# Attention units in three parts, and readers set behind their transfers, in a hybrid decoder layer

## The chip, the cores and the metric

One core of a Trainium2 chip runs the whole kernel. The metric is device time in microseconds, from the start of the program to its end. The engines are TensorE (PE, with PEld for its weight loads), VectorE (DVE), ScalarE (ACT), GpSimd (POOL) and SyncE (SP), whose queue issues almost all DMAs.

## The reference, cut to what matters

One layer for 2048 prompt rows and 64 sample rows (8 samples of 8 rows), model width 1024. A normalised row is projected once to 3584 columns. Four groups of 128 channels go through a gated MLP over chunks of 128 rows (mixer A), eight heads of 64 through an attention with three dilation patterns (mixer B). Both are normalised, gated, concatenated and projected; then a second gate is added.

```
for (w, r) in ((128, 1), (512, 4), (2048, 16)):      # window, dilation
    s = q . k * SCALE on banded blocks of 128 x 256   # rows t attend to t, t-r, ..., t-w
    p = exp(s - max(s)); den = sum(p)
    o = p @ v / den; lse = max(s) + log(den)
b_out = softmax(lse over the three patterns) . o
y = x + concat(a_out, norm(b_out) * silu(z)) @ w_out  # then a gate and a per-layer embedding
```

The samples attend in the same three patterns to a cache of 2048 rows and to their own new rows.

## The kernel before, in words

All products of the prompt are made in float16 halves: a value is split into a high half and a residual, and two or three matmuls add up their products.

**Projection.** The columns are taken in eight chunks, in the order A0, B0, B1, A1, B2, B3, A2, A3: an A chunk (384 columns) is a channel group, a B chunk (512 columns) a pair of heads. In each chunk 17 tiles of rows pass, sixteen of 128 prompt rows and as the last one the sample rows (`gemm`, L433). The sample tile keeps both halves of its rows in one tile of 128 partitions, so its product has to be folded (`fold`, L448): ScalarE copies the lower 64 rows to SBUF, a DMA moves them to the upper partitions, and VectorE adds. PSUM has three banks for these products, two for scores, two for values, one for transposes.

**Keys and queries.** Behind every fourth tile of a B chunk GpSimd normalises queries and keys (`b_norm`, L493), and `b_trans` (L532) splits them and transposes them by four DMAs from SyncE into `qk2`, one buffer for the pair of heads that is under way. The next pair may be written only when the pair before is done; the loop over tiles (L1342 to L1352) holds its groups until then, and at the eighth tile it runs the planner until `done` says so.

**Attention units.** A pair of heads has 40 units (`attn`, L642): 4 of pattern 1 and 4 of pattern 2 for each group of four tiles, and 8 of pattern 3 behind the last group, so 160 in all. A unit's first part (`scores`, L688) is two or four pairs of score matmuls, the masked maximum on VectorE (L704), the exponent on ScalarE (L712), the split in two halves on VectorE (L715, L716), and the DMA transpose of the probabilities `pc` into `pT` (L718), issued by SyncE. The second part (`stage_c`, L721) is six or twelve value matmuls (L739 to L741) and a copy by ScalarE into `rec`; a set of units (four, in pattern 3 two) fills one `rec`, which then goes to DRAM. `vload` (L628) reads the values of a set for patterns 2 and 3. `pc` and `pT` have three buffers each, `rec` two, the values three.

**Joining.** `combine` (L755) loads the three patterns' results and the gate for 512 rows, weighs them by their denominators on VectorE, ScalarE and GpSimd and stores the rows for the output phase; four joinings follow each pair of heads, as units without a second part.

**The planner.** The order of the work is written down by `Pump` (L55). It keeps a clock of its own, in ns of estimated TensorE time. Each two matmuls of a projection give it credit (0.6 ns for each ns), and it spends the credit on units: a second part when it is due, `P_LAG` (8000) behind its first part, else a first part while fewer than three wait for their second. A unit's first part is not before `QK_LAG` (3000) behind its key transposes. `later` puts a step (the mixing of an A group) at a due time. Work of the samples (`all_samples`) comes when no unit waits. `run` lets its clock run on without projections.

The framework's scheduler then makes each engine's queue from this program: it goes by the program's order, and by its own estimate of when an instruction is ready; `behind()` keeps the value matmuls behind the last projection matmul that was written ahead of them. On the chip each engine works through its queue in that order.

**Output phase.** Behind the eighth chunk 17 tiles pass through two projections of 1024 columns and one of 256 (`p3_load`, `p3_cat`, `p3_out`, `p3_gate`, `p3_ple`), with the samples' attention in between.

Of the kernel before, what the change touches and what calls it, by code (L numbers as in the profile page):

```python
# [21 lines left out]
P = 128  # L22
# [22 lines left out]
W_V3 = 3000.0  # L45
QK_LAG = 3000.0
P_LAG = 8000.0
MIX_LAG = 12000.0
# [6 lines left out]
class Pump:  # L55
# [4 lines left out]

    def __init__(self, depth, lag):
        self.depth, self.lag = depth, lag
        self.now = 0.0
        self.n = 0
        self.due = []
        self.units = []
        self.pend = []
# [9 lines left out]

    def unit(self, start, first, second):
        self.units.append((start, first, second))

# [3 lines left out]

    def _free(self):

        return self.units and (len(self.pend) < self.depth if self.units[0][2] else not self.pend)

    def _step(self):
        if self.pend and self.pend[0][0] <= self.now:  # L90
            cost = self.pend.pop(0)[1]()
        elif self._free() and self.units[0][0] <= self.now:
            _, first, second = self.units.pop(0)
            cost = first()
            if second:
                self.pend.append((self.now + cost + self.lag, second))
        elif self.units or self.pend or not self.back or self.ready > self.now:
# [22 lines left out]
    def run(self, until):  # L120
        while not until():
            if self._step() is None:
                t = []
                if self.pend:
                    t.append(self.pend[0][0])
                if self._free():
                    t.append(self.units[0][0])
                if not t:
                    assert self.back
# [6 lines left out]
def tile_hymba_gmlp_dilated_attn_step(  # L136
# [30 lines left out]
    drm = ctx.enter_context(tc.tile_pool(name="drm", bufs=1, space=DRAM))  # L167
    pump = Pump(3, P_LAG)
    uid = [0]
# [263 lines left out]
    def gemm(j, wt, ncol):  # L433
        g = pst("g", 3)
        n = 0
        for kt in range(KT):
# [3 lines left out]
            for l, r in ((lh, a), (lh, b), (xT[j][:, KT + kt], a)) if j < NT else ((lh, a), (lh, b)):  # L440
# [3 lines left out]
                if n % 2 == 0:  # L444
                    pump.tick(2 * (ncol * 0.416 + 5))
        return g if j < NT else fold(g, ncol, "tmpA")
# [191 lines left out]

    done = {}
    v_open = []  # L640

    def attn(hp, sc, grp):  # L642
# [17 lines left out]
        for pat, g, sub in steps:  # L660
            o = {}

            def first(pat=pat, g=g, sub=sub, o=o):
                if sub[0][0] == 0:
                    if pat != 1:
                        vload(hp, pat, g)
                    rec[pat] = wk.tile([P, 4, 2, RW], F32, name=nm("rec"), tag="rec", bufs=2)
                o["r"] = rec[pat]
                o["pT"], cost = scores(Q, KH, KL, o["r"], sub)
                return cost  # L670

            def second(pat=pat, g=g, sub=sub, o=o):
                with behind():
                    cost = stage_c(hp, pat, g, sub, o["r"], o["pT"])
                if pat == 1 and (sub[0][0] == 0 and g or sub[0][0] == 3 and g == 3):
                    v_open.pop(0)
                return cost
            pump.unit(start, first, second)
        if grp is None:
            for jg in range(4):  # L680
                def comb(jg=jg):
                    combine(hp, jg, sc)
                    done[hp] = jg == 3
                    return 0.0
                pump.unit(start, comb, None)


    def scores(Q, KH, KL, r, sub):  # L688
# [27 lines left out]
        nc.vector.tensor_tensor(pc[:, n:2 * n], smv, pc[:, :n], op=ALU.subtract)  # L716
        pT = wk.tile([P, 8, P], F16, name=nm("pT"), tag="pT", bufs=3)
        nc.sync.dma_start(pT[:, :2 * n // P, :], pc[:, :2 * n], transpose=True)  # L718
        return pT, 4 * ns * (kw * 0.416 + 8)

# [33 lines left out]

    def combine(hp, jg, sc):  # L755
        rows = lambda t, w: t[jg * 512:(jg + 1) * 512, 0:w].rearrange("(j p) c -> p j c", p=P)
# [5 lines left out]
        gz = wk.tile([P, 4, P], F32, name=nm("gzl"), tag="gzl", bufs=1)  # L762
        nc.sync.dma_start(gz, rows(zscr[hp], P))
        e = small(24, "e24", 2).rearrange("p (i a) -> p i a", i=3)
        nb = [t[:, :, HD + 1] for t in rr]
# [101 lines left out]
    def gemm2(o, nk, wt, m, order=((0, 0), (0, 1), (1, 0), (1, 1))):  # L867
        gs = [pst("g", 3), pst("s", 2)]
        n = [0, 0]
        for part, hf in order if m == P else ((0, 0), (0, 1)):  # L870
            for kt in range(nk):
                w = wt[(kt // 2) * 2 + hf]
                for half in range(2 - part):
# [3 lines left out]
                    if n[hf] % 2 == 0:  # L877
                        pump.tick(2 * 218.0)
        return gs if m == P else [fold(g, 512, "rl", 3) for g in gs]

# [390 lines left out]
    for _ in w0:  # L1271
        pass
    for ci, (kind, i) in enumerate(order):
        wt, sc, ncol = chunks[kind, i]
# [9 lines left out]
        for j in range(NT + 1):  # L1284
# [23 lines left out]
            if j == 6 and ci + 1 < len(order):  # L1308
                gain_load(*order[ci + 1])
            if j % 4 == 0:  # L1310
                mk = b_group if kind == "B" else a_group
                G = mk(i, j // 4, 4, P) if j < NT else mk(i, 4, 1, TS)
            g = gemm(j, wt, ncol)
# [3 lines left out]
            else:  # L1317
                for _ in range(LAST_PREP[j]):
                    if next(nxt, None):
                        break  # L1320
                if j == 14:
                    ring["cat"].append(q4t([P, D], F32, "cat"))
                    ring["x"].append(q4t([P, D], F32, "x3"))
                    p3_load(0)
                elif j == 15:
                    p3_cat(0)
            if kind == "B":
                b_evac(G, j % 4, g, sc)
            else:
                a_evac(G, j % 4, g, sc)  # L1330
            if j % 4 == 3 or j == NT:
                if kind == "B":
                    b_norm(G, sc, gch)
                    if j < NT:
                        vt[i, 1, j // 4] = G["v16"]
                        held.append((j // 4, G))
                    elif i == 3:
                        pump.back.append(all_samples())
                else:
                    a_norm(G, sc, gch)  # L1340
                    pump.later(MIX_LAG if j < NT else 2 * MIX_LAG, lambda G=G, sc=sc, gch=gch: a_mix(G, sc, gch))
            if held and j == 7:  # L1342
# [10 lines left out]
        if ci + 1 < len(order):  # L1353
            for _ in nxt:
                pass

    pump.rate = 0.5
# [61 lines left out]
```

## Time and profile before

| | |
|---|---|
| Runs | 1517.96, 1526.22, 1528.44 us; median 1526.22 us |
| Profiled execution | 1526.24 us, span 1524.5 us, granted clock 0.959 |
| TensorE busy | 1361.5 us (89%) |
| VectorE busy | 1160.8 us (76%) |
| ScalarE busy | 725.9 us (48%) |
| GpSimd busy | 538.1 us (35%) |
| Chunks end at | 112.3, 227.8, 381.1, 499.3, 629.5, 780.6, 903.1, 1018.3 us |

The span runs from the first to the last instruction; the device time has 1.7 us around it. A busy TensorE is not one at its peak: the length of a matmul depends on the clock granted to it, and ends of matmuls are modelled. SyncE has no busy time in the page; its rows tell when it issued a DMA and what it waited for before. "Idle before" is counted on the engine, and the name behind it is the last event that it waited for.

### The profile page before, as it was taken

What the parts mean: (1) busy time and instruction counts of PE and PEld (TensorE: products, weight loads), DVE (VectorE), ACT (ScalarE), POOL (GpSimd) and SP (SyncE); (2) the same over time, 40 slices, a digit from 0 to 9 for tenths busy, and PEclk for the clock granted to TensorE, in tenths of its full rate; (3) what the DMA queues carried; (4) which work ended last, traced back from release to release, by engine and by line L of the source; (5) the groups of instructions that cost most, each with busy time, mean ns of one, the idle gap of its engine ahead of it and who ended that gap; (6) DMA issues with size and microseconds to landing.
All of it is one profiled execution on the core that took longest, in us unless ns stands there. A gap on an engine that the chain in (4) does not pass through costs nothing. (4 is left out here: it accounts for less than half of the span.)

```text
span 1524.5 us, 26216 instructions
## 1 busy us (share of the span) xinstructions
PE 1361.5 (89%) x8280; PEld 693.3 (45%) x8280; DVE 1160.8 (76%) x3775; ACT 725.9 (48%) x2083; POOL 538.1 (35%) x547
## 2 busy tenths in 40 slices
PE   2989988997899988899888986788998999899998
PEld 1544544554555434455445643443343344344443
DVE  6777887588988789876999899879756675675555
ACT  6675666565656446655665544754322122221222
POOL 7123122234543654322344356643232330330101
PEclk9999999999999999999999998799999999999999
DMA  7983698588965457977697587876899799796432
GB/s 195 238 181 97 131 176 171 119 176 183 210 155 126 132 120 161 215 142 164 151 211 161 127 207 222 230 204 157 208 224 251 188 255 240 194 242 155 105 94 64
DMA packets 591436, 266.06 MB, mean 175 GB/s; under 512 B 338337, under 2 KB 568801, under 8 KB 591297
## 3 DMA queue, kind: packets, MB, share of 16 engines
q1 hardware_dynamic: 589312, 262.73, 75.4%
q0 software_dynamic: 1984, 1.66, 0.7%
q8 instruction: 65, 1.06, 0.3%
q14 instruction: 75, 0.61, 0.1%
HBM read 134.56 MB, written 48.01 MB: 120 GB/s over the span
## 5 line engine op out<-in xcount | busy, mean ns | idle before, releaser
L441 PE MATMUL psg<-wt,xT 128*128 128x512 f16 (+1 forms) x3072 | 649.6, 367 | 36.5 <-DVE agz L571 15.2
L441 PEld LDWEIGHTS <-xT 128*128 128x128 f16 x3072 | 309.9, 102 | 331.3 <-issue 60.1
L712 ACT ACTIVATE sm<-sm,rec,psc 128x256 f32<-128x256 f32 (+1 forms) x384 | 185.1, 546 | 129.4 <-DVE rec L708 103.1
L698 PE MATMUL pss<-qk 128*128 128x256 f16 (+1 forms) x384 | 132.0, 355 | 31.2 <-DMA qk<-qkc 17.2
L1126 POOL TENSOR_TENSOR K<-K,qB 96x512 f32<-96x512 f32 x64 | 88.4, 1386 | 165.8 <-DMA K<-in_cache_k_dram 70.3
L704 DVE CUSTOM_DVE_ANT_0 sm<-pss,mask 128x256 f32<-128x256 f32 (+1 forms) x384 | 122.7, 360 | 29.2 <-PE pss L699 28.1
L699 PE MATMUL pss<-qk 128*128 128x256 f16 (+1 forms) x384 | 132.8, 358 | 0.0
L874 PEld LDWEIGHTS <-Th 128*128 128x128 f16 x800 | 77.1, 99 | 109.9 <-issue 21.5
L874 PEld LDWEIGHTS <-Tc 128*128 128x128 f16 x800 | 76.4, 98 | 110.6 <-issue 19.9
L716 DVE TENSOR_TENSOR pc<-sm,pc 128x512 f16<-128x512 f32 (+1 forms) x160 | 119.0, 744 | 1.6
L963 POOL TENSOR_TENSOR tg<-tg,x 128x1024 f32<-128x1024 f32 (+1 forms) x16 | 37.6, 2347 | 183.4 <-DVE tg L962 160.4
L874 PE MATMUL psg<-w,Th 128*128 128x512 f16 x400 | 97.6, 387 | 1.2 <-DMA Th<-hl 0.5
L861 ACT ACTIVATE hl<-x,sm 128x1024 f16<-128x1024 f32 (+1 forms) x17 | 19.5, 1147 | 166.0 <-DVE sm L842 140.7
L715 DVE CAST pc<-sm 128x512 f16<-128x512 f32 (+1 forms) x160 | 80.5, 503 | 23.3 <-ACT sm L712 21.3
L874 PE MATMUL psg<-w,Tc 128*128 128x512 f16 x400 | 95.6, 379 | 2.8 <-DMA Tc<-hl 2.8
L874 PE MATMUL pss<-w,Th 128*128 128x512 f16 x400 | 94.9, 379 | 0.0
L874 PE MATMUL pss<-w,Tc 128*128 128x512 f16 x400 | 93.8, 379 | 0.0
L1127 DVE TENSOR_REDUCE blk<-K 96x8 f32<-96x512 f32 x64 | 43.0, 678 | 61.2 <-POOL K L1126 61.1
L776 POOL TENSOR_TENSOR rl<-rl,sm 128x520 f32<-128x520 f32 x48 | 55.7, 1187 | 82.9 <-ACT sm L772 80.0
L739 PEld LDWEIGHTS <-pT 128*128 128x128 f16 x600 | 57.3, 98 | 52.7 <-DMA pT<-pc 43.9
L513 POOL TENSOR_TENSOR gz<-gz,gch 128x512 f32<-128x512 f32 x16 | 20.8, 1301 | 168.9 <-DVE gz L491 83.9
L744 ACT ACTIVATE rec<-pso 128x130 f32<-128x130 f32 (+1 forms) x160 | 44.4, 295 | 46.7 <-PE pso L741 45.3
(324 smaller groups left out, 2649.5 us busy)
## 6 DMA issues: line engine op xcount, KB each, us to landing
K<-in_cache_k_dram SPq DMA_DIRECT2D x64, 192.0 KB
qB<-qd SPq DMA_DIRECT2D x64, 192.0 KB
V<-in_cache_v_dram SPq DMA_DIRECT2D x64, 192.0 KB
vt<-vscr SPq DMA_DIRECT2D x32, 258.0 KB
K<-in_cache_k_dram SPq DMA_DIRECT2D x32, 256.0 KB
V<-in_cache_v_dram SPq DMA_DIRECT2D x32, 256.0 KB
cat<-catd SPq DMA_DIRECT2D x16, 512.0 KB
x<-in_x_prompt_dram SPq DMA_DIRECT2D x16, 512.0 KB
```

The costliest lines, as they stand in the source:

```text
L441: last_mm[0] = nc.tensor.matmul(g[:, :ncol], lhsT=l, rhs=r, start=(n == 0), stop=(n == (23 if j < NT else 15)))
L698: nc.tensor.matmul(pss[:, s, h], lhsT=Q[:, h, qs], rhs=KH[:, h, ks], start=True, stop=False)
L699: nc.tensor.matmul(pss[:, s, h], lhsT=Q[:, h, qs], rhs=KL[:, h, ks], start=False, stop=True)
L704: nc.vector.tensor_tensor_reduce(sm4[:, s, h], pss[:, s, h], mk, 1.0, -3.0e38, op0=ALU.add, op1=ALU.max, accum_out=mx[:, i:i + 1])
L712: nc.scalar.activation(sm4[:, s, h], sm4[:, s, h], AF.Exp, bias=r[:, sl + s, h, HD + 1:HD + 2], scale=psc)
L715: nc.vector.tensor_copy(pc[:, :n], smv)
L716: nc.vector.tensor_tensor(pc[:, n:2 * n], smv, pc[:, :n], op=ALU.subtract)
L739: nc.tensor.matmul(po[:, s, h, 0:65], lhsT=H, rhs=v[:, vs_, a:a + 65], start=(bi == 0), stop=False)
L744: nc.scalar.activation(r[:, sl:sl + ns, :, 0:65], po[:, :ns, :, 0:65], AF.Copy)
L776: nc.gpsimd.tensor_tensor(ti, ti, e[:, i, :].unsqueeze(2).to_broadcast([P, 8, 65]), op=ALU.mult)
L874: last_mm[0] = nc.tensor.matmul(gs[hf], lhsT=o[part][:, kt], rhs=w[:, kt % 2, half, :], start=(n[hf] == 0), stop=(n[hf] == (3 if m == P el ...
L1126: nc.gpsimd.tensor_tensor(K3, K3, qB, op=ALU.mult)
```

## The change

Units have three parts: scores; the transposes (`mid`), due `P_LAG` behind the scores; values, due `T_LAG` behind the transposes. Three units may be open between the first two parts and three more between the last two. `P_LAG` goes from 8000 to 5500, `T_LAG` is 5500, `QK_LAG` goes from 3000 to 9000. A unit that begins a set has to wait in the planner until fewer than two sets and fewer than three loads of values are open. A joining is no unit any more: its loads come `R_LAG` (6000) behind the values of the pair's last unit, its work 6000 behind its loads, and the next joining's loads 6000 behind that. `done` is set with the last scores of a pair. The sample tile's fold is cut in two: the add and all that follows it come `T_LAG` behind the copy and its DMA. Ahead of the first output tile the planner runs until the last pair is joined, and behind the last chunk until its sample rows are folded.

```diff
-QK_LAG = 3000.0
-P_LAG = 8000.0
+QK_LAG = 9000.0
+P_LAG = 5500.0
+T_LAG = 5500.0
+R_LAG = 6000.0
...
+    def unit(self, start, free, first, mid, second):
+        self.units.append((start, free, first, mid, second))
+    def _free(self):
+        return self.units and len(self.made) < self.depth and self.units[0][1]()
-    def _free(self):
-        return self.units and (len(self.pend) < self.depth if self.units[0][2] else not self.pend)
     def _step(self):
+        while self.made and self.made[0][0] <= self.now and len(self.pend) < self.depth:
+            _, mid, second = self.made.pop(0)
+            mid()
+            self.pend.append((self.now + self.lag2, second))
         if self.pend and self.pend[0][0] <= self.now:
             cost = self.pend.pop(0)[1]()
         elif self._free() and self.units[0][0] <= self.now:
-            _, first, second = self.units.pop(0)
+            _, _, first, mid, second = self.units.pop(0)
             cost = first()
-            if second:
-                self.pend.append((self.now + cost + self.lag, second))
+            self.made.append((self.now + cost + self.lag, mid, second))
...
     def fold(g, n, tag, bufs=2):
         c = wk.tile([P, 512], F32, name=nm("fold"), tag=tag, bufs=bufs)
         nc.scalar.activation(c[TS:, :n], g[TS:, :n], AF.Copy)
         nc.sync.dma_start(c[:TS, :n], c[TS:, :n])
-        nc.vector.tensor_tensor(c[:TS, :n], c[:TS, :n], g[:TS, :n], op=ALU.add)
-        return c
+        def end():
+            nc.vector.tensor_tensor(c[:TS, :n], c[:TS, :n], g[:TS, :n], op=ALU.add)
+            return c
+        return end
...
             def first(pat=pat, g=g, sub=sub, o=o):
                 if sub[0][0] == 0:
+                    r_open.append((pat, g))
                     if pat != 1:
+                        vt_open.append((pat, g))
                         vload(hp, pat, g)
...
+                if grp is None and sub[0][0] == 2 and g == 3:
+                    done[hp] = True
+                o["pc"], o["n"], cost = scores(Q, KH, KL, o["r"], sub)
+            def mid(o=o):
+                o["pT"] = wk.tile([P, 8, P], F16, name=nm("pT"), tag="pT", bufs=3)
+                nc.sync.dma_start(o["pT"][:, :2 * o["n"] // P, :], o["pc"][:, :2 * o["n"]], transpose=True)
             def second(pat=pat, g=g, sub=sub, o=o):
...
+                if sub[-1][0] == 3:
+                    r_open.remove((pat, g))
+                    for k in [(2, g - 1)] * (pat == 2 and g > 0) + [(pat, g)] * (pat == 3 or pat == 2 and g == 3):
+                        vt_open.remove(k)
+                if grp is None and sub[0][0] == 2 and g == 3:
+                    pump.later(R_LAG, lambda: comb(0))
-            pump.unit(start, first, second)
-        if grp is None:
-            for jg in range(4):
-                def comb(jg=jg):
-                    combine(hp, jg, sc)
-                    done[hp] = jg == 3
-                    return 0.0
-                pump.unit(start, comb, None)
+            free = (lambda: len(r_open) < 2 and len(vt_open) < 3) if sub[0][0] == 0 else lambda: True
+            pump.unit(start, free, first, mid, second)
+        def comb(jg):
+            got = comb_load(hp, jg)
+            def work():
+                combine(hp, jg, sc, *got)
+                if jg < 3:
+                    pump.later(R_LAG, lambda: comb(jg + 1))
+                else:
+                    joined[hp] = True
+            pump.later(R_LAG, work)
...
                 if j == 14:
+                    pump.run(lambda: joined.get(3))
...
+            if j == NT:
+                def end(f=fold(g, ncol, "tmpA"), sc=sc, gch=gch, kind=kind, i=i):
+                    G = (b_group if kind == "B" else a_group)(i, 4, 1, TS)
...
+                    folded[kind, i] = True
+                pump.later(T_LAG, end)
+                continue
...
+    pump.run(lambda: folded.get(order[-1]))
```

`gemm2` of the output phase calls the two halves of the fold for both halves of the columns in turn: both copies and DMAs first, then both adds. `comb_load` holds the four loads that stood at the head of `combine`.

## Rows read from the trace of the kernel before

**Rows 1.** The page, part 1: busy us (share of the span) and instructions.

```profile
PE 1361.5 (89%) x8280; PEld 693.3 (45%) x8280; DVE 1160.8 (76%) x3775; ACT 725.9 (48%) x2083; POOL 538.1 (35%) x547
```

**Rows 2.** Busy time by stretches; the last columns are granted clock, DMA share, GB/s.

```profile
core 0: us, PE busy (x) PEld busy (x) DVE busy (x) ACT busy (x) POOL busy (x), PEclk, DMA share, GB/s
112.30:903.10 790.80, 717.10 (x5011) 396.85 (x5010) 652.31 (x2377) 453.53 (x1399) 299.72 (x335) 0.95 0.73 158
903.10:1018.30 115.20, 87.06 (x472) 47.75 (x469) 99.10 (x269) 64.70 (x208) 71.59 (x61) 0.88 0.76 216
1018.30:1450.00 431.70, 413.21 (x2067) 174.51 (x2067) 288.26 (x734) 114.25 (x264) 117.31 (x80) 0.99 0.88 202
381.10:499.30 118.20, 109.30 (x836) 67.43 (x835) 102.54 (x378) 69.94 (x222) 52.57 (x49) 0.93 0.72 162
```

**Rows 3.** TensorE's waits, 112.3 to 903.1 us: in total, times, longest (us).

```profile
PE pso L739 <- DMA pT<-pc: 32.1, 23, 4.3
PE pss L698 <- DMA qk<-qkc: 17.2, 8, 3.6
PE pss L698 <- DVE sm L704: 13.6, 16, 1.7
PE psg L441 <- DVE gz L491: 4.6, 1, 4.6
...
PE psg L441 <- DVE fold L453: 1.0, 1, 1.0
```

**Rows 4.** One unit, 617 to 624 us, timelines of VectorE, SyncE, TensorE: start, us.

```profile
617.60 0.68 DVE L716 TENSOR_TENSOR pc<-sm,pc 128x512 f16<-128x512 f32 x1
...
617.17 1.42 SPq L551 DMA_TRANSPOSE qk<-qkc  x1
618.69 1.25 SPq L718 DMA_TRANSPOSE pT<-pc  x1
...
623.51 0.24 PE L739 MATMUL pso<-vt,pT 128*128 128x65 f16 x1 [2.88 <-DMA pT<-pc]
```

**Rows 5.** SyncE: its waits, whole span; L718's durations (ns), first, last (us).

```profile
SPq L718 <- DVE pc L716: 106.4, 68, 5.1
...
SPq L634 <- PE pso L741: 34.0, 7, 6.4
...
L718 SPq DMA_TRANSPOSE pT<-pc x160: 1188/1234/3514, 153.7 to 891.8; - x160
```

**Rows 6.** VectorE's waits for transfers, 100 to 1020 us.

```profile
DVE sm L767 <- DMA rl<-r2d: 11.2, 11, 3.3
...
DVE fold L453 <- DMA fold<-fold: 7.1, 5, 3.0
DVE sm L768 <- DMA rl<-r3d: 6.4, 6, 3.1
```

**Rows 7.** Stretches with a lowered clock; columns as in Rows 2.

```profile
268.00:292.30 24.30, 24.30 (x158) 13.28 (x157) 14.66 (x73) 13.07 (x41) 8.01 (x10) 0.86 0.61 140
278.70:282.10 3.40, 3.40 (x10) 1.28 (x9) 3.10 (x14) 3.40 (x13) 3.12 (x6) 0.50 0.41 80
623.40:626.80 3.40, 3.29 (x22) 2.09 (x23) 2.87 (x14) 1.79 (x6) 0.18 (x1) 0.50 1.14 260
```

**Rows 8.** VectorE's work for units, by line: busy us, mean ns; idle before.

```profile
L704 DVE CUSTOM_DVE_ANT_0 sm<-pss,mask 128x256 f32<-128x256 f32 (+1 forms) x384 | 122.7, 360 | 29.2 <-PE pss L699 28.1 <-issue 0.3
L716 DVE TENSOR_TENSOR pc<-sm,pc 128x512 f16<-128x512 f32 (+1 forms) x160 | 119.0, 744 | 1.6
L715 DVE CAST pc<-sm 128x512 f16<-128x512 f32 (+1 forms) x160 | 80.5, 503 | 23.3 <-ACT sm L712 21.3 <-DMA pT<-pc 0.9 <-DMA kd<-sb 0.2
L708 DVE TENSOR_SCALAR rec<-sm,nsc 128x2 f32<-128x2 f32 (+1 forms) x160 | 54.5, 353 | 10.4 <-DMA r2d<-rec 5.9 <-DMA r3d<-rec 2.4 <-DMA r1d<-rec 1.7
L704 DVE DVE_READ_ACCUMULATOR2_ANT sm<- 128x1 f32 x384 | 31.4, 82 | 0.0
```

More of the change, by code (lines that the diff above doesn't have):

```diff
@@ L66, in __init__ @@
         self.units = []
+        self.made = []
         self.pend = []
@@ L92, in _step @@
         elif self._free() and self.units[0][0] <= self.now:
-            _, first, second = self.units.pop(0)
+            _, _, first, mid, second = self.units.pop(0)
             cost = first()
-            if second:
-                self.pend.append((self.now + cost + self.lag, second))
-        elif self.units or self.pend or not self.back or self.ready > self.now:
+            self.made.append((self.now + cost + self.lag, mid, second))
+        elif self.units or self.made or self.pend or not self.back or self.ready > self.now:
             return None
@@ L122, in run @@
             if self._step() is None:
-                t = []
-                if self.pend:
-                    t.append(self.pend[0][0])
+                t = [q[0][0] for q in (self.due, self.pend) if q]
+                if self.made and len(self.pend) < self.depth:
+                    t.append(self.made[0][0])
                 if self._free():
                     t.append(self.units[0][0])
-                if not t:
-                    assert self.back
+                if self.back and not (self.units or self.made or self.pend):
                     t.append(self.ready)
@@ L639, in tile_hymba_gmlp_dilated_attn_step @@
     done = {}
+    r_open = []
+    vt_open = []
+    joined = {}
     v_open = []
@@ L716, in scores @@
         nc.vector.tensor_tensor(pc[:, n:2 * n], smv, pc[:, :n], op=ALU.subtract)
-        pT = wk.tile([P, 8, P], F16, name=nm("pT"), tag="pT", bufs=3)
-        nc.sync.dma_start(pT[:, :2 * n // P, :], pc[:, :2 * n], transpose=True)
-        return pT, 4 * ns * (kw * 0.416 + 8)
+        return pc, n, 4 * ns * (kw * 0.416 + 8)
     def stage_c(hp, pat, grp, sub, r, pT):
@@ L763, in combine @@
         nc.sync.dma_start(gz, rows(zscr[hp], P))
+        return rr, gz
+    def combine(hp, jg, sc, rr, gz):
         e = small(24, "e24", 2).rearrange("p (i a) -> p i a", i=3)
@@ L878, in gemm2 @@
                         pump.tick(2 * 218.0)
-        return gs if m == P else [fold(g, 512, "rl", 3) for g in gs]
+        return gs if m == P else [f() for f in [fold(g, 512, "rl", 3) for g in gs]]
     S = {}
@@ L1326, in tile_hymba_gmlp_dilated_attn_step @@
                     p3_cat(0)
+            if j == NT:
+                def end(f=fold(g, ncol, "tmpA"), sc=sc, gch=gch, kind=kind, i=i):
+                    G = (b_group if kind == "B" else a_group)(i, 4, 1, TS)
+                    if kind == "B":
+                        b_evac(G, 0, f(), sc)
+                        b_norm(G, sc, gch)
+                        if i == 3:
+                            pump.back.append(all_samples())
+                    else:
+                        a_evac(G, 0, f(), sc)
+                        a_norm(G, sc, gch)
+                        pump.later(MIX_LAG, lambda: a_mix(G, sc, gch))
+                    folded[kind, i] = True
+                pump.later(T_LAG, end)
+                continue
             if kind == "B":
@@ L1330, in tile_hymba_gmlp_dilated_attn_step @@
                 a_evac(G, j % 4, g, sc)
-            if j % 4 == 3 or j == NT:
+            if j % 4 == 3:
                 if kind == "B":
                     b_norm(G, sc, gch)
[L1334 to L1338, printed above, removed]
+                    vt[i, 1, j // 4] = G["v16"]
+                    held.append((j // 4, G))
                 else:
                     a_norm(G, sc, gch)
-                    pump.later(MIX_LAG if j < NT else 2 * MIX_LAG, lambda G=G, sc=sc, gch=gch: a_mix(G, sc, gch))
+                    pump.later(MIX_LAG, lambda G=G, sc=sc, gch=gch: a_mix(G, sc, gch))
             if held and j == 7:
```

19 lines of the change are left out of this document (8 added, 11 removed).

## The prediction

> **What bounds the kernel now.** I read the busy shares first: TensorE is busy for 89% of the span and VectorE for 76%, so the matmuls are the bound and 163 us of TensorE's span (1524.5 - 1361.5) is idle [rows 1]. The second look is where that idle time lies, by stretches. From the end of the first projection chunk to the end of the seventh, which is where all the attention runs, TensorE is busy 717.1 of 790.8 us: 73.7 us idle, and the granted clock is 0.95 there; the eighth chunk adds 28.1 us of idle time, and most of the output phase 18.5 us in 431.7 [rows 2]. The other 43 us of the 163 lie in the head and the tail, which the change does not touch. The third look is what ended those 73.7 us. The list of TensorE's waits names two transfers first: the value matmuls wait for the DMA transpose of the probabilities (32.1 us in 23 waits, the longest 4.3 us), and the score matmuls wait for the transposed keys (17.2 us in 8). Next come scores that wait for VectorE to empty a score bank (13.6 us in 16), and projections that wait for VectorE's evacuations (a few us) [rows 3]. The chain of waits reaches back only over the last 33 us and says nothing about the middle.
>
> One unit shows how the first wait comes about [rows 4]: VectorE ends the residual half at 618.28 us, SyncE is still issuing a key transpose and gets to this unit's transpose at 618.69 us, and the values start at 623.51 us, 4.8 us after that issue began, with TensorE idle for 2.88 us. The planner thought that 8 us behind the scores were enough. SyncE is a queue of its own here: issuing one of the 160 transposes takes 1.2 us, and it stood waiting for VectorE's half in front of them for 106 us, and 34 us in front of loads of values for a buffer that was still being read [rows 5].
>
> **The change, part by part.** Durations are of the profiled execution, 1526.24 us, which is the median of the three runs (1526.22) to within 0.1 us, so the sum is made against either.
>
> **1. Units in three parts.** In the planner's time the values came one score cost (4 x (256 x 0.416 + 8) = 458 ns) plus 8000 ns after the scores, 8.46 us. Now it is 458 + 5500 + 5500 = 11.46 us: 3.0 us more for the same chain. Nothing is added on any engine; 160 transposes stand later in the program, 6 us behind their scores, and at that place VectorE's half is mostly done, so SyncE should block less. The mean wait is 1.4 us (32.1 / 23) and the longest 4.3 us: if 3.0 us came off each, nearly all would go, -32 at most. If the transposes really left 5.5 us later than now, the gain would be 0, or a loss of up to 2.5 us for a unit (the second rival below). The nearest rows are those of the unit above, whose transpose left 0.4 us behind VectorE's end; it can leave no earlier in either version, and 3.0 us would have covered its 2.88 us. I take -22, two thirds of 32.1, since DMA is busy 0.73 of this stretch [rows 2] and flights will still vary.
>
> **2. Key readers 9 us behind the key transposes, not 3.** The waits are 2.2 us each (17.2 / 8), the longest 3.6 us, and 6 us more cover each one: -17 at most. The projection goes on meanwhile and hides the delay; without projection tiles it would cost 6 us for each of 16 groups, but at least a whole chunk of them follows each group. A key transpose also has to get through SyncE (1.42 us of it in rows 4), so I take -13, three quarters; the other end is 0.
>
> **3. Loads of the joining, the sample rows' sums.** VectorE stood at the head of its queue for 11.2 + 6.4 us until loads of the three partial results had landed, and for 7.1 us until the sample rows had been moved down [rows 6]: 24.7 us during which nothing behind could run. All these instructions stay, as do the 64 loads of the joining; they are issued 6 us ahead of their readers. What it is worth to TensorE depends on who waits for VectorE: 13.6 + 4.6 + 1.0 us in the attention stretch [rows 3]. Between 0 and -25 I take -8, a third of what VectorE gets back. The sample tile's PSUM bank is held for 5.5 us more; three banks rotate, and the next tile but one, which wants it, comes two projection tiles later (by the planner's cost 24 x (384 x 0.416 + 5) = 3950 ns a tile). Cost 0, covered by these tiles; were the cover gone, 1.0 us, the one such wait in rows 3, at each of 8 chunks: +8.
>
> **4. Order of heads.** "done" is now set with the last scores, not behind four joinings that each waited until no unit was pending. The next pair's key transposes come earlier and the units spread over more projection tiles. Only order changes: 0. The new wait for the joining of the last pair (ahead of the fifteenth tile of the last chunk) lies near 903.1 + 115.2 x 15 / 17 = 1005 us [rows 2], over 110 us behind the last unit's transpose at 891.8 us [rows 5], and four joinings at two lags of 6 us need 48: 0. What stands behind it in the program is the load for the first output tile; the planner's clock alone runs on.
>
> **5. Clock.** A clock of 0.95 over 790.8 us costs up to 39.5 us [rows 2]. The granted clock is at half (1.2 instead of 2.4 GHz) right from the end of the 2.88 us wait above; but it is so at 278.7 us too, within a stretch of 24.3 us in which TensorE was busy throughout [rows 7]. So not all of it comes from waits. Steps 1 and 2 take away 35 of 73.7 us of idle time; in proportion that is 39.5 x 35 / 73.7 = 18.7 us, and because of the falls without a wait I take three quarters, -14 (ends 0 and -36). The Trainium skill ("TensorE: Matmul & The Clock Gate", "HAM oscillation — how this bites in real kernels") puts the half rate down to idle gaps at TensorE; the fall behind the 2.88 us wait agrees, the one at 278.7 us does not. By that rule alone the term would be -18.7 and the time 1476 us.
>
> **6. New waits.** The first part of a unit no longer waits for its values. Units could come every (458 + 5500) / 3 = 1.99 us, were it not for the credit: 0.6 ns for each ns of projection, and a unit of 458 + 432 = 890 ns needs 1483 ns of it, one unit in 2.37 us. Before, three units in 8.46 us made it 2.82 us. VectorE's work for one unit is 2 x 360 + 2 x 82 + 353 + 503 + 744 = 2484 ns [rows 8]: while units are backed up, VectorE is the slower. The two score banks are then full more often, and the row for that, 0.85 us each (13.6 / 16), gives the price: I take 14 more such waits, +12 (ends 0 and +54).
>
> Sum: -22 - 13 - 8 - 14 + 12 = -45, so 1526 - 45 = **1481 us**.
>
> **The rivals.** *VectorE becomes the bound (slower).* In the fourth chunk (381.1 to 499.3 us) VectorE is already busy 102.5 of 118.2 us [rows 2]. If the faster supply of units makes half of the 160 wait 0.85 us for their score bank, that is 68 - 13.6 = 54 us more; against -22 - 13, with nothing from the clock or from VectorE's own waits, it comes to +19: 1545 us. It decides from 57 such waits on (16 + 35 / 0.85), in place of 16. For it speaks 2484 ns against 2370; against it, that keys for eight units come only with every fourth projection tile, so that units are backed up in a part of the time only, and that VectorE's total does not grow.
>
> *Still late (no change).* The kernel's final order is made by a scheduler that issues what is ready first in its own estimate of time. A transpose that stands later in the program may be issued where it was, and then the change of places does nothing but move the values, or it may leave later by as much as the values do, and the 32.1 us stay. Clock and new waits then cancel, and -13 - 8 + 12 leave 1517 us; if one unit in twenty also loses 2.5 us on a later transpose, 20 us more, 1537. The transpose in rows 4 took 4.8 us from its issue with other transfers in flight, and the issue itself was held up by a key transpose.
>
> "DMA: Bandwidth & Descriptors" of the Trainium skill ("Queues, rings and completion order") says that each DMA engine takes up SyncE's descriptors in ring order. By that rule a transpose issued later stands behind whatever was issued before it, and the time is this rival's 1517 us; rows 4 agree as far as they go.
>
> *More than the sum (faster).* If all of 32.1 + 17.2 us goes with its whole share of the clock (39.5 x 49.3 / 73.7 = 26 us) and VectorE's 8 us, and nothing new comes: -83, 1443 us.
>
> **How the numbers follow.** The sum has 0.55 (1455 to 1508 by the ends of its smaller terms), more than the sum 0.13, still late 0.19 (1505 to 1537), VectorE 0.13. Predicted: 1481 us. From 1440 to 1538 us some 0.05 is left out below and 0.09 above. One per cent is 15 us, about what can be told from no change in this kernel. Faster by more than that: 0.55 + 0.13 + 0.02 of "still late" = 0.70; within it the other 0.17; slower 0.13.
>
> **What would show it.** Right: the value matmuls' wait for the transposes under 12 us, the keys' under 5, VectorE's waits for the loads of the joining gone, idle time of TensorE in the attention stretch from 74 to near 40 us, clock there 0.96 to 0.97. Wrong: SyncE's transposes leaving several us behind VectorE's half; scores waiting for VectorE over 40 us; the same number of waits on the transposes with new lengths; or the attention stretch shorter and the eighth chunk or the output phase longer by as much.

## The result, and the profile after

The changed kernel takes 1539.88 us (median, 1538.66 to 1541.47) beside 1527.33 us for the kernel before: a ratio of 1.0103, 95% interval 1.0079 to 1.0127. It is slower by one per cent where 1481 us were forecast. The profiled execution took 1540.82 us, span 1539.1, granted clock 0.949 (before 0.959).

The page, part 1, as in [rows 1]:

```profile
PE 1371.6 (89%) x8280; PEld 694.6 (45%) x8280; DVE 1147.1 (75%) x3775; ACT 724.3 (47%) x2083; POOL 538.9 (35%) x547
```

The span grew by 14.6 us. The same 8280 matmuls kept TensorE busy 10.1 us longer (1371.6 - 1361.5), at a lower granted clock, and its idle time went from 163.0 to 167.5 us, 4.5 more. So two thirds of the loss are matmuls at a lower clock, and the idle time that the change was to take away is all there. By stretches (columns as in [rows 2], the attention, the eighth chunk, most of the output phase):

```profile
112.00:913.90 801.90, 727.02 (x5015) 398.24 (x5014) 662.65 (x2414) 452.77 (x1401) 318.42 (x347) 0.94 0.75 161
913.90:1035.50 121.60, 89.12 (x469) 48.19 (x467) 87.41 (x238) 64.36 (x207) 64.64 (x56) 0.86 0.64 187
1035.50:1450.00 414.50, 396.07 (x1997) 167.29 (x1996) 267.62 (x699) 108.65 (x254) 103.73 (x72) 0.98 0.87 205
```

The attention stretch has 74.9 us of idle time (73.7 before) and 9.9 us more of busy time at 0.94; the eighth chunk is 6.4 us longer. The waits of TensorE in the attention stretch, as [rows 3]:

```profile
PE pso L769 <- DMA pT<-pc: 27.6, 23, 3.4
PE pss L730 <- DVE sm L736: 16.2, 13, 4.3
PE pss L730 <- DMA qk<-qkc: 11.1, 9, 3.7
PE pst L610 <- ACT vhl L596: 5.3, 1, 5.3
PE pss L730 <- DVE gch L1281: 3.5, 1, 3.5
```

The two waits that the change aimed at are still the first and third of the list: 27.6 us where 32.1 stood, in the same number of waits, and 11.1 where 17.2 stood. New single waits of 5.3 and 3.5 us stand beside them. VectorE's waits for transfers (100 to 1037 us), as [rows 6], did not go but grew, from 24.7 to 34.0 us:

```profile
DVE sm L801 <- DMA rl<-r3d: 20.7, 11, 3.2
...
DVE sm L800 <- DMA rl<-r2d: 7.3, 7, 2.8
DVE fold L461 <- DMA fold<-fold: 6.0, 4, 3.0
```

Only one row of SyncE shows what was meant. In front of the transposes it waited less for VectorE's half than in [rows 5] (the row here is of 100 to 1037 us, where all 160 lie):

```profile
SPq L690 <- DVE pc L748: 77.7, 46, 7.3
```

Over all rows of this line SyncE's waiting in front of the transposes fell only from 223.6 to 204.0 us.

Two chunks show how the time is lost, the fifth and the seventh; before:

```profile
499.30:629.60 130.30, 112.66 (x651) 55.23 (x650) 113.90 (x375) 65.24 (x202) 67.97 (x73) 0.93 0.66 147
780.70:903.10 122.40, 108.73 (x858) 67.78 (x856) 107.69 (x383) 67.89 (x228) 57.58 (x63) 0.96 0.78 171
```

and after:

```profile
496.00:628.80 132.80, 114.00 (x650) 55.60 (x649) 116.01 (x384) 64.55 (x204) 71.28 (x73) 0.91 0.64 144
784.40:913.90 129.50, 112.96 (x830) 68.57 (x829) 114.64 (x399) 66.91 (x224) 66.23 (x72) 0.91 0.78 180
```

In the seventh chunk the clock falls from 0.96 to 0.91, and busy and idle time both grow. In the eighth chunk of the changed kernel the timeline of TensorE has two long gaps (start, length, instruction, and in brackets the idle time before it with what ended it):

```profile
955.24 1.11 PE L1139 MATMUL pst<-ident,K 128*128 128x128 f32 x4 [6.18 <-DVE sb L620]
...
972.82 2.08 PE L447 MATMUL psg<-wt,xT 128*128 128x384 f16 x6 [6.23 <-DVE agz L580]
```

The key transposes of the samples wait for the one transpose bank, which a mixing group holds until VectorE has read it; then a projection waits for VectorE's evacuation. Neither has to do with a unit's transposes, the last of which was issued at 888 us: other steps meet here.

### The profile page after: what moved, and what is told of

Read it like the earlier page. It is cut to its first block, busy times and chain, and to the rows that moved or that the text cites. A ratio compares the mean times of both kernels' runs of the same rounds, so it can differ in the third digit from the quotient of the medians.

```text
span 1539.1 us, 26248 instructions
## 1 busy us (share of the span) xinstructions
PE 1371.6 (89%) x8280; PEld 694.6 (45%) x8280; DVE 1147.1 (75%) x3775; ACT 724.3 (47%) x2083; POOL 538.9 (35%) x547
## 5 line engine op out<-in xcount | busy, mean ns | idle before, releaser
L447 PE MATMUL psg<-wt,xT 128*128 128x512 f16 (+1 forms) x3072 | 659.9, 371 | 39.6 <-DVE agz L580 25.1
L730 PE MATMUL pss<-qk 128*128 128x256 f16 (+1 forms) x384 | 132.7, 357 | 30.9 <-DVE sm L736 16.2
L736 DVE CUSTOM_DVE_ANT_0 sm<-pss,mask 128x256 f32<-128x256 f32 (+1 forms) x384 | 122.2, 359 | 18.1 <-PE pss L731 16.1
L907 PEld LDWEIGHTS <-Tc 128*128 128x128 f16 x800 | 77.2, 98 | 105.8 <-issue 13.7
L748 DVE TENSOR_TENSOR pc<-sm,pc 128x512 f16<-128x512 f32 (+1 forms) x160 | 123.2, 770 | 1.6
L996 POOL TENSOR_TENSOR tg<-tg,x 128x1024 f32<-128x1024 f32 (+1 forms) x16 | 37.5, 2346 | 214.5 <-DVE tg L995 170.3
L747 DVE CAST pc<-sm 128x512 f16<-128x512 f32 (+1 forms) x160 | 87.4, 546 | 22.1 <-ACT sm L744 18.4
L769 PE MATMUL pso<-vt,pT 128*128 128x65 f16 x352 | 41.6, 195 | 26.6 <-DMA pT<-pc 22.7
```

What stands on the lines that cost most here:

```text
L447: last_mm[0] = nc.tensor.matmul(g[:, :ncol], lhsT=l, rhs=r, start=(n == 0), stop=(n == (23 if j < NT else 15)))
L730: nc.tensor.matmul(pss[:, s, h], lhsT=Q[:, h, qs], rhs=KH[:, h, ks], start=True, stop=False)
L736: nc.vector.tensor_tensor_reduce(sm4[:, s, h], pss[:, s, h], mk, 1.0, -3.0e38, op0=ALU.add, op1=ALU.max, accum_out=mx[:, i:i + 1])
L747: nc.vector.tensor_copy(pc[:, :n], smv)
L769: nc.tensor.matmul(po[:, s, h, 0:65], lhsT=H, rhs=v[:, vs_, a:a + 65], start=(bi == 0), stop=False)
L907: last_mm[0] = nc.tensor.matmul(gs[hf], lhsT=o[part][:, kt], rhs=w[:, kt % 2, half, :], start=(n[hf] == 0), stop=(n[hf] == (3 if m == P el ...
```

## The experiments

Ratios are to the kernel before, run beside each, with a 95% interval. Letters in the expectations: A, the three parts (in the later texts, the change) have a price of their own; B, the joinings cost where they are spread beside other work; C, any new order redraws the stalls, so that a time is one draw out of many; D, denser units use up the longer lag; F, it is VectorE's general lateness; Q, the queue that the scheduler makes sets the distance between scores and values; L, the planned lag sets it.

**One part alone, or all but one.** All four parts undone in the new planner, and each part alone:

```diff
# n0_none: the changed kernel, all parts set back
-P_LAG = 5500.0
+P_LAG = 0.0
-    pump = Pump(3, P_LAG, T_LAG)
+    pump = Pump(3, P_LAG, 8000.0)
+        return ... len(self.made) + len(self.pend) < self.depth ...
# a1_keys9: the kernel before
-QK_LAG = 3000.0
+QK_LAG = 9000.0
# a2_fold: the kernel before
+T_LAG = 5500.0
+                pump.later(T_LAG, end)          # the sample tile's add and what follows
# a3_join: the kernel before
+            got = comb_load(hp, jg)
+            pump.later(R_LAG, work)
# a4_parts: the changed kernel with all but the three parts and the limits on sets set back
-QK_LAG = 9000.0
+QK_LAG = 3000.0
+                pump.unit(start, lambda: not (pump.made or pump.pend), comb, None, None)
# b4_parts0: the changed kernel without the three parts and the limits on sets (rest kept)
```

In all but a1, as in the changed kernel, due steps also set the planner's clock where it runs on without projections; n0 shows what that does by itself.

> All four parts of the change undone in the new planner (two-part units, lag 8, keys 3 us behind, joinings as units, fold in place). It differs from the kernel before only in that due steps also set the planner's clock where it runs on without projections, which shifts the order slightly from the first joining on. Theory A (the three parts themselves cost the time) and theory B (the joinings, spread beside the samples, cost it): ratio 1.000 +- 0.003. Theory C (any new order re-rolls the stalls): off by 0.004 or more either way.

> The key readers' lag alone, 9 us for 3. By the prediction's step 2 the score matmuls' wait for key transposes goes from 17 to under 5 us: ratio 0.988 to 0.993. By theory C (each new order re-rolls the stalls) 0.993 to 1.010 with 10 us or more of that wait left or as much added elsewhere.

> The sample rows' sums alone, 5.5 us behind their transfer. By the prediction's step 3: 2 to 4 us less, ratio 0.997 to 0.999. By theory C 0.993 to 1.010.

> The joinings alone (loads 6 us ahead, next joining 6 us behind, the pair free for the next one with its last scores); units, keys and fold as before. Theory A: ratio 0.997 to 1.001. Theory B: 1.006 to 1.010, with the loss in the seventh and eighth chunk. Theory C: anywhere from 0.99 to 1.01.

> The three-part units and the limits on open sets alone (5.5 + 5.5 us, six open), the rest as before. Theory A: ratio 1.007 to 1.012, with bursts of units that VectorE works off late and waits of the values as many as before. Theory B: 0.990 to 1.000. Theory C: anywhere from 0.99 to 1.01 without a relation to the run that has all but this part.

> The changed kernel with two-part units again (transposes with the scores, values 8 us behind, three open, no limits on sets); keys 9 us, joinings and fold as changed. Theory A: ratio 1.000 or less (0.995 to 1.001). Theory B: 1.008 to 1.012, the loss in the seventh and eighth chunk kept. Theory C: no relation to the run with this part alone.

| | ratio | TensorE's wait on transposes, us | on keys, us |
|---|---|---|---|
| n0_none | 0.9997 [0.9978, 1.0016] | 25.4 | 19.7 |
| a1_keys9 | 1.0090 [1.0054, 1.0126] | 37.5 | 5.5 |
| a2_fold | 1.0133 [1.0105, 1.0161] | 19.6 | 9.6 |
| a3_join | 1.0073 [1.0050, 1.0096] | 33.2 | 17.2 |
| a4_parts | 1.0102 [1.0076, 1.0128] | 30.8 | 14.0 |
| b4_parts0 | 1.0172 [1.0142, 1.0201] | 38.5 | 11.7 |

The parts don't add: alone they come to +0.90, +1.33, +0.73 and +1.02, together 4.0 per cent, and all of them at once cost 1.0. Theory A's price for the three parts fits a4, but without them the change costs more, not less. B's ratio fits a3, but not its place: the seventh and eighth chunks of a3 take 235.9 us together, 237.7 before; and b4 lies above what B allowed. C missed too: n0, for which it wanted 0.004 or more of difference, came out as A and B had it, and a2 lies above its 1.010. The waits move on their own: the transposes' wait is lowest (19.6 us) where only the sample tile's fold is moved, and that kernel is 1.3 per cent slower all the same. Its loss lies in the output phase, 525.1 us for 506.2, with 9.6 us more of idle time and 9.4 more of busy time (columns as in [rows 2]; a2 behind the eighth chunk, then the kernel before):

```profile
1015.70:1540.80 525.10, 491.02 (x2384) 206.22 (x2382) 321.32 (x811) 132.41 (x295) 124.62 (x83) 0.98 0.76 177
1018.30:1524.50 506.20, 481.67 (x2383) 205.34 (x2382) 328.55 (x819) 132.46 (x295) 124.33 (x83) 0.99 0.80 184
```

There the samples' key transposes wait for ScalarE's copies (TensorE's waits of a2 from 1020 us on; before, 7.3 us in 3 waits):

```profile
PE pst L1107 <- ACT KT L1117: 22.0, 5, 6.5
```

**Lag and spacing in the kernel before.** A longer lag with three units open, and first parts at least 2.8 us apart:

```diff
# c1_lag11
-P_LAG = 8000.0
+P_LAG = 11000.0
# c3_even
+        elif self._free() and max(self.units[0][0], self.first_at) <= self.now:
+            self.first_at = self.now + 2800.0
```

> The kernel before with the values 11 us behind their scores in place of 8, still three units open: the planner's distance of the changed kernel (11.5 us) without its closer units (three in 11.5 us, before three in 8.5, changed three in 6). Theory D (the change's 3 us were eaten by units that come closer, which VectorE works off late): the value matmuls wait under 15 us for their transposes (before 32), ratio 0.985 to 0.997. Theory F (the waits go with VectorE's lateness in general, whatever the lag): 25 to 35 us of them, ratio 0.997 to 1.010.

> The kernel before with first parts of units at least 2.8 us apart in the planner's time, where now three come at once and none for 8 us: the same number of units per time, evenly spread. Theory D: VectorE gets to each unit sooner, transposes wait under 20 us, scores for VectorE under 8 (before 13.6), ratio 0.985 to 0.997. Theory F: waits as before, ratio 0.997 to 1.005.

c1: 1.0418 [1.0387, 1.0449]; c3: 1.0041 [1.0016, 1.0066]. The longer lag did not shorten the waits on the transposes but made them the most of all kernels here:

```profile
PE pso L739 <- DMA pT<-pc: 47.6, 39, 3.2
```

Its planner has to run on without projections for 109 us of its own time (12 before) to get the units through, so units stand where no projection covers them: in TensorE's queue the least projection between a unit's scores and its values is 0.0 us (5.0 before). c3 has 24.3 us of these waits and 21.5 of scores waiting for VectorE, together what before had. D falls with c1: units planned 12 us apart by threes are not denser than before, and no wait is covered. F's 25 to 35 us and its 1.010 are passed by c1 as well; only c3's ratio is as F had it.

**Neighbours: the same kernel in another order.** First the kernel before, samples' steps some 3 and 6 us later in the planner's time:

```diff
# s1_samp3 (s2_samp6: 2300.0)
+        yield 0.0, 1150.0
# r1_lag81, r3_lag78, r5_lag82: P_LAG 8100, 7800, 8200 in the kernel before
# r2_lag54, r4_lag56, r6_lag53: P_LAG/T_LAG 5400/5600, 5600/5400, 5300/5700 in the changed kernel
```

> The kernel before, with one thing moved: the samples' steps get 1150 ns less of the planner's credit at their start, so they come about 3 us later in the program; no step is added or removed, and all that is written ahead of them (the attention) keeps its order. Theory C (a new order shifts the samples' key transposes against the evacuations and the output tiles, and that alone moves the time): a ratio to the kernel before anywhere from 0.997 to 1.015, with the attention's chunks the same within 2 us each and the difference in the eighth chunk and the output phase. Theory A (each part of the change has a cost of its own; order alone does nothing): 0.998 to 1.002, output phase 506 us within 3.

> As the run before it, with 2300 ns less credit, so that the samples' steps come about 6 us later. Theory C: again 0.997 to 1.015, and not the same as with 3 us (the two differ by more than 0.003, in no set direction). Theory A: 0.998 to 1.002, and the same as with 3 us.

> The kernel before with P_LAG 8100 in place of 8000: values 0.1 us later in the planner, far too little to cover or uncover any wait by itself (the mean wait on a transpose is 1.4 us). It only changes which step comes next at some places. Theory C: 0.997 to 1.012, chunks of the attention differ from before's by up to 7 us either way. Theory A: 0.998 to 1.002.

> The changed kernel with P_LAG 5400 and T_LAG 5600 in place of 5500 and 5500: the values keep their place in the planner's time, the transposes leave 0.1 us earlier. Theory A: 1.010 +- 0.002, as the changed kernel. Theory C: within 0.01 of the changed kernel's ratio on either side, chunk lengths differing by several us from the changed kernel's, so that the 1.0 per cent is one draw and not the price of the change.

> The kernel before with P_LAG 7800 in place of 8000 (7900 gives the same order of instructions as 8000). Theory C (the order is a draw): a ratio of 1.000 to 1.015 to the kernel before. Theory A (the change has a price, the kernel before none): 0.998 to 1.004, below the changed kernel's 1.010.

> The kernel before with P_LAG 8200. Theory C: 1.000 to 1.015, and not ordered with the lag (8100 gave 1.0135). If a longer lag with three units open is what costs (as 11000 did with 1.042): above 8100's ratio, 1.014 or more.

> The changed kernel with P_LAG 5600 and T_LAG 5400. Theory C: anywhere from 1.000 to 1.020; with the neighbours of before, the two sets overlap. Theory A: 1.010 +- 0.002, or above the highest neighbour of before.

> The changed kernel with P_LAG 5300 and T_LAG 5700: the transposes leave 0.2 us earlier, the values where they were. Theory C: anywhere from 1.000 to 1.020. Theory A: 1.010 +- 0.003. If earlier transposes are what costs (5400 gave 1.0195): above 1.0195.

The times of the engines are of one profiled execution of each kernel; idle is its span less TensorE's busy time, and the last column goes to the end of the eighth chunk.

| | ratio | TensorE busy, us | idle, us | wait on transposes, us |
|---|---|---|---|---|
| before, lag 8000 | 1 | 1361.5 | 163.0 | 32.1 |
| lag 7800 | 1.0163 [1.0138, 1.0188] | 1374.6 | 176.8 | 41.8 |
| lag 8100 | 1.0135 [1.0097, 1.0174] | 1372.7 | 170.1 | 28.2 |
| lag 8200 | 1.0015 [0.9994, 1.0035] | 1361.6 | 159.5 | 26.7 |
| samples 3 us later | 1.0057 [1.0034, 1.0081] | 1372.0 | 167.1 | 31.3 |
| samples 6 us later | 1.0084 [1.0057, 1.0112] | 1370.1 | 165.9 | 30.8 |
| changed, 5500/5500 | 1.0103 [1.0079, 1.0127] | 1371.6 | 167.5 | 27.6 |
| 5400/5600 | 1.0195 [1.0155, 1.0234] | 1369.8 | 179.3 | 35.6 |
| 5600/5400 | 1.0045 [1.0022, 1.0067] | 1359.8 | 166.7 | 33.0 |
| 5300/5700 | 1.0157 [1.0131, 1.0182] | 1370.6 | 172.1 | 29.5 |

A lag moved by 0.1 or 0.2 us can't cover or uncover a wait of 1.4 us, and it is not even the direction that decides: 7800 and 8100 cost 1.6 and 1.4 per cent, 8200 nothing. So an order alone moves the time, as C says and A denies. How far, C did not say rightly: 8100 and 7800 lie a little above its 1.012 and 1.015, the two runs of the samples differ by 0.0027 where it wanted more than 0.003, and n0 did not move. The four lags of the kernel before average 1.0078, the four of the changed kernel 1.0125; with standard deviations of 0.8 and 0.65 per cent the difference is 0.5 per cent, with a 95% interval of -0.8 to +1.8. So the two sets overlap, and the change by itself is worth nothing that these runs can tell; the 2.9 per cent forecast are outside. The kernel before is the lowest of its own set. (Lags near each other are taken here as independent draws; that is an assumption. The busy and idle times hang on one execution each: that of the samples 3 us later is the slowest of its ten, 1541.18 us where their median is 1533.64.)

**The planned distance, far to either side.**

```diff
# q1_lag4: the kernel before
-P_LAG = 8000.0
+P_LAG = 4000.0
# q2_lag16: the changed kernel (its fold stays at 5500)
-P_LAG = 5500.0
-T_LAG = 5500.0
+P_LAG = 8000.0
+T_LAG = 8000.0
```

> The kernel before with P_LAG 4000: values planned 4.9 us behind their scores (median), not 8.8; projection written in between 3.4 us, but in TensorE's queue 9.7 (before 10.2). Theory Q (the scheduler's queue sets the distance, the planned lag does not reach it): waits of the value matmuls on the transposes 25 to 45 us, within the spread of the neighbours, and a ratio of 0.995 to 1.02. Theory L (the planned lag is what covers the transposes, as the forecast took it): 3.9 us more wait at most of the 160 units, so over 150 us of such waits and a ratio above 1.08.

> The changed kernel with P_LAG and T_LAG 8000 (the sample tile's fold keeps its 5.5 us): values planned 16.9 us behind their scores, projection written in between 11.9 us, in TensorE's queue 10.2. Theory Q: waits on the transposes 25 to 45 us again. Theory L: under 8 us, since 5 us more than the changed kernel covers even its longest wait (3.4 us). The time tells little: the planner runs 77 us without projections here (5.5 in the changed kernel), which costs up to 2 per cent either way of it.

q1: 1.0117 [1.0042, 1.0191]; q2: 1.0247 [1.0183, 1.0310]. TensorE's waits on the transposes, 112 to 914 us, of q1, where L forecast over 150 us:

```profile
PE pso L739 <- DMA pT<-pc: 32.1, 27, 3.3
```

and of q2, where L forecast under 8:

```profile
PE pso L769 <- DMA pT<-pc: 27.4, 27, 3.5
```

Planned distances of 4.8 and 8.8 us give the same 32.1 us, 11.8 and 16.9 give 27.6 and 27.4 (and c1's 11.7 gave 47.6). Why, is seen in the queues of the built kernels: the projection work between a unit's last score matmul and its first value matmul, mean of 160 units in us of the planner's cost, as the program writes it and as it stands in TensorE's queue; and, from the traces, the time on the chip from VectorE's maxima of a unit (`rec<-sm,nsc`) to the copy of its values (median, us):

| | planned distance (median) | written | in the queue | on the chip |
|---|---|---|---|---|
| q1_lag4 | 4.8 | 3.4 | 9.7 | 12.8 |
| before | 8.8 | 6.7 | 10.2 | 13.3 |
| c1_lag11 | 11.7 | 8.4 | 9.6 | 13.2 |
| changed | 11.8 | 8.9 | 10.3 | 13.6 |
| q2_lag16 | 16.9 | 11.9 | 10.2 | 13.7 |

Both scores and values stand behind their place in the program (before: scores 9.3, values 12.7 us of projection on average; changed: 10.4 and 11.8), and a longer written distance is paid back by a smaller shift of the values against the scores (queue less written, from the top of the table down: 6.3, 3.5, 1.2, 1.4 and -1.7 us). Q holds: from 4.8 to 16.9 us of planned distance the queue has 9.6 to 10.3, and the lag reaches it only as another draw. Why it is some 10 us, and not another number, no run shows; that the scheduler's estimate of readiness sets it is argued.

Which units wait is not told by the queue either. With units matched in order, the first on each engine with the first, from a unit's last score matmul to the end of VectorE's half it is 11.4 us on average in the 23 units that waited before and 9.6 in the other 137 (changed: 11.2 and 10.2), while the projection between scores and values is 9.6 us and 10.3 (changed: 10.5 and 10.2). So a unit waits where VectorE's half came late; why it came late there was not followed.

## Why the prediction was wrong

**Step 1** failed, with the largest term (-22; measured 32.1 to 27.6, -4.5, and nothing in the mean of neighbours: 32.2 in the four lags of the kernel before, 31.4 in those of the changed one). The working took the planner's 3.0 us as 3.0 us on the chip; in TensorE's queue the distance went from 10.2 to 10.3 us, and on the chip the copy of a unit's values came 0.3 us later. The unit of [rows 4] was read rightly, but its values stood where the scheduler had put them. The transposes did not leave 5.5 us later: from the end of VectorE's half to their issue it is 0.08 us before and 0.57 after (median; more than 1 us in 42 units before, in 59 after). The mechanism, that a planned place need not be the place in the queue, was written down in the rival "still late", a scheduler that goes by its own estimate, with a chance of 0.19. That rival's 1517 us were too low, since it kept steps 2 and 3 as gains, and these pass through the same scheduler. That rival took from the ring order in "DMA: Bandwidth & Descriptors" of the Trainium skill ("Queues, rings and completion order") that a transpose issued later stands behind what was issued before it. No run shows that order itself; the transposes took much the same time: in the units that waited for theirs, it is 3.8 us from its issue to the first value matmul before and 4.1 after (mean of 23 each).

**Step 2** (-13): the waits went from 17.2 to 11.1 us, -6. With the key lag alone they were 5.5 us, near the forecast's "under 5", but then the transposes' waits rose to 37.5 and the time by 0.9 per cent. And q1, with the old key lag, had 7.9. Over all kernels here the wait on keys averages 13.7 us at a key lag of 3 us (13 kernels, 6.7 to 19.7) and 9.8 at 9 us (7 kernels, 5.5 to 13.0): the lag may be worth some 4 us of this wait, not 13, and no gain in time shows it.

**Step 3** (-8): nothing. VectorE's waits grew to 34.0 us; here too the planned distance did not arrive. From the issue of a joining's last load to its first reader it is 4.2 us before and 3.7 after (median of 16), from the fold's DMA to its add 4.2 and 3.5 (of 8), where the planner had put 6.0 and 5.5 us in between. The held PSUM bank cost next to nothing: one wait of a projection on the fold, of 1.4 us (1.0 in [rows 3]).

**Step 4** (0) was mis-sized. "Only order changes: 0" is the step that the neighbours refute: an order alone is worth 0 to 1.6 per cent. Where the time is lost moves with it: the eighth chunk of the changed kernel, 121.6 us, is 113.7, 113.6 and 123.0 us in its three neighbours (5400, 5600 and 5300), and the output phase behind it, 503.6 us, is 520.0, 507.8 and 502.0.

**Step 5** (-14) went the other way, +10.1 us of busy time for the same matmuls. It was tied to idle time, which did not go; but the tie fails too. By its ratio (39.5 / 73.7) 4.5 us more of idle time would make some 2 us of busy time (an estimate), and a2 has 16.1 us more of busy time than before at the same idle time (163.2 us). A fall with TensorE busy on both sides, as at 688.0 us (last section), is one that no shorter wait takes away.

**Step 6** (+12): 13.6 to 16.2 us, +2.6 (neighbours after 19.2 to 23.7), inside its ends. "VectorE becomes the bound" did not happen: VectorE was busy 13.7 us less, not more, and scores waited 13 times, not 57. The sign of that rival came true without its mechanism.

By the forecast's own list: the transposes' wait over 12 us, the keys' over 5, the joining's waits still there, the idle time not near 40 and the clock 0.94, so none of the five came true; the sign "the same number of waits with new lengths" is what came, 23 and 23.

What stays open: which meeting of steps costs how much in each draw. It was followed only for single gaps (the eighth chunk above, the key copies of a2). That the one per cent of the changed kernel lies within what an order does is shown by the spread of its neighbours, not by the steps themselves. That the longer busy time is the clock's is read from the same count of matmuls at a lower granted clock; why the clock fell at each place was not tested. No version tried is faster than the kernel before; the nearest are n0 (0.9997) and lag 8200 (1.0015).

## What to carry to other kernels

Before a lag in a planner is priced, count its distance in the engine's queue of the built kernel: where a scheduler re-orders by its own estimate, a planned distance may not arrive there at all. Before a change of order of about one per cent is believed, gain or loss, time two or three neighbours that differ in nothing that matters; here they spread over 1.6 per cent for the kernel before (1 to 1.0163) and 1.5 for the changed one (1.0045 to 1.0195), and a single comparison with a tight interval says which order won, not which idea.

## What the runs showed of the hardware

The clock fell to half (1.2 GHz) with TensorE busy throughout by its modelled ends, as in [rows 7], here behind a run of pattern 3 scores and narrow value matmuls of the changed kernel; ahead of it the engine had no gap either:

```profile
684.60:688.00 3.40, 3.40 (x25) 2.27 (x22) 1.98 (x13) 0.65 (x4) 0.00 (x0) 1.00 0.66 141
688.00:691.40 3.40, 3.40 (x11) 1.30 (x10) 0.00 (x0) 0.00 (x0) 0.00 (x0) 0.50 0.50 171
```

VectorE's residual split of the output weights takes 0.74 us at the median and up to 1.78 (minimum, median and maximum in ns, 36 of them):

```profile
L864 DVE SCALAR_TENSOR_TENSOR w<-w3st,sm,w x36: 723/737/1782, 952.2 to 1084.3; 128x512 f16<-128x512 f32 x36
```

Five of the six slow ones stand in the eighth chunk beside GpSimd's products and adds of the joining, ahead of a wait of TensorE for VectorE's evacuation. VectorE, 996 to 1004 us, the splits alone:

```profile
994.46 3.00 DVE L864 SCALAR_TENSOR_TENSOR w<-w3st,sm,w 128x512 f16<-128x512 f32 x2
997.99 2.89 DVE L864 SCALAR_TENSOR_TENSOR w<-w3st,sm,w 128x512 f16<-128x512 f32 x2
1002.25 2.06 DVE L864 SCALAR_TENSOR_TENSOR w<-w3st,sm,w 128x512 f16<-128x512 f32 x3
```

and GpSimd meanwhile:

```profile
992.94 3.98 POOL L809 TENSOR_TENSOR rl<-rl,sm 128x520 f32<-128x520 f32 x3 [4.62 <-ACT sm L805]
996.88 3.44 POOL L811 TENSOR_TENSOR rl<-rl,rl 128x520 f32<-128x520 f32 x2
1000.40 1.37 POOL L814 TENSOR_TENSOR rl<-rl 128x512 f32<-128x512 f32 x1
```

"SBUF — State Buffer" of the Trainium skill ("SBUF: two separate sides") says that a VectorE operation with two inputs in SBUF and a GpSimd operation that reads SBUF take one port pair in turn, each for its whole length. These rows agree: the five splits that begin while one of these GpSimd operations runs (the first at 993.51 us, ahead of these rows) take 1.03 to 1.78 us, and each ends 0.54 or 0.55 us behind the end of such an operation; the three from 1002.25 us on, behind the last, take 0.74 us each. The same is seen ahead of the 6.23 us gap at 972.82 us above. There three products of the joining on GpSimd

```profile
969.28 3.08 POOL L809 TENSOR_TENSOR rl<-rl,sm 128x520 f32<-128x520 f32 x3
```

run beside steps of VectorE that are 128x4 in size, and the evacuation for which TensorE waits (L580) stands behind these in VectorE's queue:

```profile
970.39 0.97 DVE L190 TENSOR_TENSOR sm<-sm 128x4 f32<-128x4 f32 x1
971.40 0.98 DVE L191 TENSOR_TENSOR sm<-sm,sm 128x4 f32<-128x4 f32 x1
972.41 0.16 DVE L192 SCALAR_TENSOR_TENSOR sm<-sm 128x4 f32<-128x4 f32 x1
972.49 0.28 DVE L580 SCALAR_TENSOR_TENSOR agz<-th,psg 128x128 f32<-128x128 f32 x1
```

A joining's place therefore costs VectorE time too, and here TensorE as well, which no step of the forecast had.
